# Two transformer-like layers on one core: the residual stream with tokens on the partitions

## The chip, the cores and the metric

The kernel runs on one core of a Trainium2 chip. The metric is the time of one execution on the device in microseconds; lower is better. The time before is the median of three runs. A core has TensorE (PE) for matrix products, VectorE (DVE), ScalarE (ACT) and GpSimd (POOL) for work on tiles, SyncE (SP), which here only issues transfers, and 16 DMA engines move data between device memory (DRAM) and the on-chip buffer. Each engine works through its own list of instructions in order.

## The reference

Input `x` is 512 tokens of width 1024 in fp32; two layers run one after the other. What matters here:

```
def rms_norm(x, g):
    y = x * rsqrt(mean(x * x, axis=-1) + 1e-6)
    return y * g
mod = cond @ mod_w + mod_b            # 6 x 1024 per layer
shift1, scale1, gate1, shift2, scale2, gate2 = split(mod, 6)
h = rms_norm(x, attn_pre_g) * (1 + scale1) + shift1
proj = h @ w_in                       # to four mixers A, B, C, D
y = concat([y_a, y_b, y_c, y_d]) @ w_out
x = x + gate1 * rms_norm(y, attn_post_g)
h = rms_norm(x, mlp_pre_g) * (1 + scale2) + shift2
y = square(relu(h @ mlp_w1)) @ mlp_w2         # 1024 -> 4096 -> 1024
x = x + gate2 * rms_norm(y, mlp_post_g)
```

The mixers are sparse attention with a top-k choice of keys (A), retention (B), gated linear attention (C) and differential attention (D). Each norm is over the 1024 values of one token.

## The kernel before

Every fp32 matrix is split on the chip into a high part (a cast on ACT to a shortened fp32) and a low part (a subtraction on DVE or POOL), and every product is three matmuls (`mm3`, lines 268 to 270). `prep` (line 254) loads a weight tile of 256 KB through SP, casts it (line 262) and subtracts (line 264).

A layer has two functions. `mixers` projects `h` and runs A to D; its output is `yv`, with the width on the partitions, eight tiles of 128 x 512 tokens. `rest` (from line 1231) does everything behind: the output projection (products named `po`), the post-norm and the residual, the pre-norm, and the MLP in four quarters of 1024 hidden channels: `pf` is the first matrix of a quarter, `p2` (shown in the profile as `p`) the second, which adds up in the tiles `y`. The first quarter's `pf` and the whole of the last quarter's `p2` work in two halves of 256 tokens, all else on 512.

The residual `x` and all `y` have the width on the partitions, too: tile `i` holds channels 128 i to 128 i + 127 for all tokens. Then a norm's sum over the width goes across partitions. `SumSq` (line 443) squares each tile on ACT, adds the squares on DVE or POOL into a few partial sums, and adds those over the partitions by a matmul with a matrix of ones (line 467, `sspost` and `sspre`); its result has the sum on all partitions, and `rstd` makes the factor from it on 128 x 256 values. `residual` updates `x`, `prenorm` and `normed` make the normed `h` (lines 510 to 515), in steps that the code places between the products of the next half. `xsave` holds `x` in DRAM while the next layer's mixers use its space.

The modulation `cond @ mod_w` is a list of matrix-vector products on DVE, each with a tile of 512 KB (`gw`, line 281), kept in `todo`; `fill(n)` takes the next n of them at points in the code. `gain` (line 301) combines their results with a norm's weight, 128 x 8 numbers with the width on the partitions.

A list scheduler sets the order of each engine's instructions at build time, from the code's order and its own costs; the table `PLAN` holds choices for it, such as which engine takes a low part. On the chip an instruction starts when the one ahead of it on its engine and its inputs are done.

The lines that the change replaces first of all:

```
ps = yp.tile([P, HT], F32, name="ss" + self.name, tag="yp")
for i, q in enumerate(self.all):
    pe.matmul(ps, ones, q, start=i == 0, stop=i == len(self.all) - 1)
```

Of the kernel before, what the change touches and what calls it, by code (L numbers as in the profile page):

```python
# [39 lines left out]
 'fA': {},  # L40
# [49 lines left out]
P = 128  # L90
L = 2
# [106 lines left out]
def tile_trunk(ctx: ExitStack, tc: tile.TileContext, a, out, dbg=None):  # L198
# [110 lines left out]
    xsave = nc.dram_tensor("xsave", (P, KT, T), F32, kind="Internal").ap()  # L309
# [133 lines left out]
    class SumSq:  # L443

        def __init__(self, name):
            self.n, self.name = 0, name
            self.acc = {}
            self.all = []

        def add(self, t):  # L450
            k = PLAN["sq"][self.n:self.n + 1]
            new = k in "T" or k not in self.acc
            if new:
                q = nt.tile([P, HT], F32, name=f"sa{self.name}{self.n}", tag="sa", bufs=4)
                self.all.append(q)
                self.acc[k] = q
            else:
                q = nt.tile([P, HT], F32, name=f"sq{self.name}{self.n}", tag="sq")
            act.activation(q, t, AF.Square)  # L459
            if not new:  # L460
                (pool if k == "P" else dve).tensor_tensor(self.acc[k], self.acc[k], q, ALU.add)  # L461
            self.n += 1

        def total(self):
            ps = yp.tile([P, HT], F32, name="ss" + self.name, tag="yp")
            for i, q in enumerate(self.all):
                pe.matmul(ps, ones, q, start=i == 0, stop=i == len(self.all) - 1)  # L467
            return ps

# [4 lines left out]
    def h_tiles(name):  # L474
        return [tuple(hp.tile([P, T], F32R, name=f"{name}{i}{s}", tag="h" + s, bufs=KT) for s in "hl") for i in range(KT)]
# [6 lines left out]
    def chain(*gens):  # L482
        for g in gens:
            yield from g

    def step(g, n):
        for _ in range(n):
            next(g, None)

    def residual(l, which, y, ss, half, nxt=None):  # L490

        name = f"{which}{l}_{half}"
        c = cs(half)
        r = rstd(ss.total(), name)
        yield
        g = gmul[l, which]
# [902 lines left out]
```

## Time and profile before

| | |
|---|---|
| three runs | 1503.92, 1506.04, 1510.22 us, median 1506.04 |
| the profiled execution | 1500.35 us |
| its span, first to last instruction | 1498.6 us |
| TensorE busy | 1424.6 us, 95% |
| VectorE busy | 990.7 us, 66% |
| ScalarE busy | 742.3 us, 50% |
| GpSimd busy | 280.5 us, 19% |
| mean granted TensorE clock | 0.981 of full speed |

All views below are of that one profiled execution; times in them count from the first instruction. A name such as `po<-yT_6l,whi` is the tile written and the tiles read, without their numbers; `<-` behind an idle time names what ended it. In the view by stage the busy times stand in the order PE, PEld (TensorE's weight load), DVE, ACT, POOL. "Granted clock" is the share of TensorE's full speed that the chip gave. The stretches of the program, read from the names in the timeline: start and first projections 0 to 55 us, mixers of layer 0 to 330, output projection to 387, first `pf` to 439, the rest of the MLP to 712, the last quarter's `p2` to 764, first projections of layer 1 to 810, its mixers to 1068, output projection to 1118, first `pf` to 1171, the rest of the MLP to 1437, the last quarter's `p2` to 1485, and the end.

### The profile page before, as it was taken

To read this page: it belongs to the slowest core of one execution; us is meant where nothing else is said; L and a number is where in the kernel's file an instruction comes from. 1 tells how busy PE (TensorE), PEld (TensorE's weight loads), DVE (VectorE), ACT (ScalarE), POOL (GpSimd) and SP (SyncE) were. 2 spreads that over 40 slices of the span, in tenths; PEclk is the share of its full clock that TensorE was granted. 3 is DMA by queue.
4 is the path that set the end of the run, shared out by engine and by line. 5 is a ranking of instruction groups with operands and counts; after the bars stand their busy time and mean duration, and the time that the engine had idled before them with its cause. 6 is when DMAs were issued, how large, how long until landed. Compare 5 with 4: busy or idle time off the path is not lost.

```text
span 1498.6 us, 23592 instructions
## 1 busy us (share of the span) xinstructions
PE 1424.6 (95%) x8514; PEld 1190.9 (79%) x8514; DVE 990.7 (66%) x2209; ACT 742.3 (50%) x1655; POOL 280.5 (19%) x268
## 2 busy tenths in 40 slices
PE   7989999999999999999989899999999999999996
PEld 4667878768898878888978769787789888888896
DVE  8798878786796875434477999753678334343435
ACT  4667486656453323324257575855765333242322
POOL 3244321335100000000032443213430000000001
PEclk8999999999999999999999999999999999999999
DMA  9420223466078884333131102211531433333301
GB/s 340 140 68 14 78 71 99 150 205 222 29 245 288 294 268 155 92 99 92 43 113 59 57 15 72 71 43 56 163 104 52 126 93 94 97 97 93 94 20 57
DMA packets 82269, 171.12 MB, mean 114 GB/s; under 512 B 9284, under 2 KB 16102, under 8 KB 81896
## 3 DMA queue, kind: packets, MB, share of 16 engines
q1 hardware_dynamic: 79524, 167.47, 35.7%
q10 hardware_dynamic: 2628, 2.14, 0.4%
q8 instruction: 67, 1.10, 0.3%
q14 instruction: 50, 0.41, 0.1%
HBM read 165.39 MB, written 4.19 MB: 113 GB/s over the span
## 4 chain that ended last, share of the span: by engine, by line
PE 71%; DVE 17%; ACT 4%; DMA 4%; issue 2%; POOL 1%; SPq 0%; DVEq 0%; ACTq 0%; POOLq 0%
PE p L269 7%; PE p L270 7%; PE p L268 7%; PE pf L269 7%; PE pf L270 7%; PE pf L268 7%; PE ptm L268 3%; PE ptm L269 3%; PE ptm L270 3%; DVE ia L797 2%; DVE m L810 2%; DVE ia L811 2%; PE first L1186 1%; DMA gw<-modw 1%; PE firstk L1186 1%
## 5 line engine op out<-in xcount | busy, mean ns | idle before, releaser
L262 ACT CAST whi<-raw 128x512 fp32r<-128x512 f32 x388 | 237.3, 621 | 355.9 <-PE p L269 157.9
L264 DVE TENSOR_TENSOR wlo<-raw,whi 128x512 fp32r<-128x512 f32 x266 | 190.8, 722 | 205.7 <-ACT whi L262 194.1
L264 POOL TENSOR_TENSOR wlo<-raw,whi 128x512 fp32r<-128x512 f32 x122 | 165.1, 1371 | 330.0 <-ACT whi L262 279.7
L461 POOL TENSOR_TENSOR sapost<-sapost,sqpost 128x256 f32<-128x256 f32 x16 | 12.3, 771 | 671.6 <-ACT sqpost L459 671.6
L281 DVE CUSTOM_DVE_ANT_0 gw<-gw,cond 128x1024 f32<-128x1024 f32 x80 | 101.3, 1269 | 40.6 <-DMA gw<-modw 40.2
L810 DVE MAX8 m<-ia 128x8 f32<-128x256 f32 (+2 forms) x96 | 53.1, 556 | 1.3
L811 DVE MATCH_REPLACE8 ia<-m,ia 128x256 f32<-128x256 f32 (+2 forms) x96 | 52.0, 542 | 0.0
L914 ACT COPY QF<-q 32x256 f32<-32x256 f32 x120 | 48.4, 403 | 5.5 <-DVE q L891 2.5
L1288 DVE TENSOR_TENSOR rf<-rf,pf 128x512 f32<-128x512 f32 (+1 forms) x80 | 45.8, 574 | 2.6 <-ACT rf L1287 2.5
L1287 ACT ACTIVATE rf<-pf 128x512 f32<-128x512 f32 (+1 forms) x80 | 40.5, 507 | 5.6 <-PE pf L270 5.6
L923 PE MATMUL sg<-QF,KF 128*64 128x256 f32 x224 | 30.5, 395 | 11.0 <-DVE AC L929 8.2
L602 DVE CUSTOM_DVE_ANT_0 sD<-sd,msk 128x128 f32<-128x128 f32 (+3 forms) x64 | 29.6, 488 | 16.8 <-PE sd L1021 12.0
L604 ACT ACTIVATE sD<-sD,mnD 128x128 f32<-128x128 f32 (+3 forms) x64 | 35.5, 559 | 6.8 <-DVE mnD L602 6.4
L890 POOL TENSOR_TENSOR KF<-F,kc 128x512 f32<-128x512 f32 x16 | 23.9, 1502 | 43.7 <-ACT F L883 42.4
L268 PE MATMUL p<-hd_7h,whi 128*128 128x512 f32 (+1 forms) x80 | 28.6, 358 | 3.1 <-ACT hd_7h L471 3.1
L923 PEld LDWEIGHTS sg<-QF,KF 128*64 128x64 f32 x224 | 14.6, 137 | 21.0 <-issue 13.7
L269 PE MATMUL pf<-h_5l,whi 128*128 128x512 f32 (+1 forms) x80 | 28.0, 350 | 2.8 <-DVE h_5l L515 2.8
L797 DVE SCALAR_TENSOR_TENSOR ia<-rl,wi,ia 128x256 f32<-128x256 f32 (+2 forms) x42 | 29.0, 708 | 2.2 <-ACT rl L791 1.0
L269 PE MATMUL p<-hd_7l,whi 128*128 128x512 f32 (+1 forms) x80 | 28.3, 353 | 0.6 <-DVE hd_7l L472 0.6
L268 PE MATMUL ptm<-whi,h_0h 128*128 128x256 f32 x74 | 25.4, 345 | 3.5 <-ACT h_0h L511 3.5
L467 PE MATMUL sspre<-sapre,ones 128*128 128x256 f32 x48 | 17.3, 474 | 12.0 <-POOL sapre L461 7.1
L268 PE MATMUL p<-hd_0h,whi 128*128 128x512 f32 (+1 forms) x80 | 28.4, 355 | 0.0
(623 smaller groups left out, 5002.2 us busy)
## 6 DMA issues: line engine op xcount, KB each, us to landing
raw<-w SPq DMA_DIRECT2D x256, 256.0 KB, 2.7
gw<-modw SPq DMA_DIRECT2D x80, 512.0 KB, 4.2
raw<-wtm SPq DMA_DIRECT2D x76, 256.0 KB, 2.8
gs<-modw SPq DMA_DIRECT2D x16, 512.0 KB, 6.3
raw<-wo SPq DMA_DIRECT2D x32, 256.0 KB, 2.7
raw<-wtc SPq DMA_DIRECT2D x24, 256.0 KB, 2.8
xin<-xT SPq DMA_DIRECT2D x8, 256.0 KB, 3.5
wq<-wtm SPq DMA_DIRECT2D x8, 256.0 KB, 6.4
```

Source lines behind the costliest of these rows:

```text
L262: act.copy(hi, raw)
L264: (lo_eng or dve).tensor_tensor(lo, raw, bits(hi), ALU.subtract)
L268: pe.matmul(ps, l[0], r[0], start=start, stop=False)
L269: pe.matmul(ps, l[0], r[1], start=False, stop=False)
L270: pe.matmul(ps, l[1], r[0], start=False, stop=stop)
L281: return dve.tensor_tensor_reduce(raw, raw, cond, 1.0, 0.0, ALU.mult, ALU.add, modT[l][:, c:c + 1])
L797: e.scalar_tensor_tensor(t, rl, wi[:, b, hd:hd + 1], t, ALU.mult, ALU.add)
L810: dve.max(m8, acc)
L811: dve.match_replace(acc, m8, acc, MARK)
L914: f(Q[r, :, hd, :], QS4[c // 2][r, 2 * (c % 2):2 * (c % 2) + 2, :])
L923: pe.matmul(ps[t, i], KF[:, lv, t], Q[:, i, :, t], start=True, stop=True)
L1288: dve.tensor_tensor(rl, rl, ps, ALU.mult)
```

## The change

`x` and `y` now have the tokens on the partitions: four blocks of 128 tokens by 1024. The output projection and `p2` use a block of activations as the operand that stands still, and a row of weights of 512 columns as the one that moves; the weights lie in DRAM accordingly. A norm's sum is then along the free dimension: ACT squares two halves of 512 and sums them in the same instruction (`rsqrt_mean`), and the factor is one number a partition. The post-norm's gain has to lie along the free dimension, the same on all partitions: `gain_row` writes the 128 x 8 numbers to DRAM and reads them back as a row for all partitions. What the projections and `pf` need is still the width on the partitions: `turn_block` transposes a normed block on TensorE, eight pieces of 128 x 128, and ACT applies gain and shift while reading the result. `h` is one tile for all eight width tiles (two with the low part). The matrix-vector products that stood in the output projection of layer 0 are emptied ahead of it, eight of them by the plan's entry `fA` within the mixers.

```
- 'fA': {},
+ 'fA': {'2': 2},
...
-    o["wo"] = f("w_out").reshape(L, 2, 4, P, KT, P).transpose(0, 4, 1, 3, 2, 5)
+    o["wo"] = f("w_out").reshape(L, KT, P, 2, T).transpose(0, 3, 1, 2, 4)
...
-    o["w2"] = f("mlp_w2").reshape(L, 4, 2, 4, P, KT, P).transpose(0, 1, 5, 2, 4, 3, 6)
+    o["w2"] = f("mlp_w2").reshape(L, 4, KT, P, 2, T).transpose(0, 1, 4, 2, 3, 5)
...
     def h_tiles(name):
-        return [tuple(hp.tile([P, T], F32R, name=f"{name}{i}{s}", tag="h" + s, bufs=KT) for s in "hl") for i in range(KT)]
+        a, b = (hp.tile([P, KT, T], F32R, name=f"{name}{s}", tag="h" + s, bufs=1) for s in "hl")
+        whole[name] = (a, b)
+        return [(a[:, i], b[:, i]) for i in range(KT)]
...
+    def rsqrt_mean(halves, name):
+        ss = tiny("ss" + name, 2)
+        for c in range(2):
+            junk = nt.tile([P, T], F32, name=f"jk{name}{c}", tag="nm_r", bufs=1)
+            act.activation(junk, halves[c], AF.Square, accum_out=ss[:, c:c + 1])
+        m = tiny("ms" + name)
+        dve.tensor_tensor(m, ss[:, 0:1], ss[:, 1:2], ALU.add)
+        dve.tensor_scalar(m, m, 1.0 / DM, EPS, ALU.mult, ALU.add)
+        r = tiny("rs" + name)
+        act.activation(r, m, AF.Ln)
+        act.activation(r, r, AF.Exp, scale=-0.5)
+        t = tiny("tt" + name)
+        dve.tensor_tensor(t, r, r, ALU.mult)
+        dve.scalar_tensor_tensor(t, t, -0.5, m, ALU.mult, ALU.mult)
+        dve.scalar_tensor_tensor(r, t, 1.5, r, ALU.add, ALU.mult)
+        return r
...
+    def gain_row(l, which):
+        g = gmul[l, which]
+        row = nt.tile([P, DM], F32, name=f"row_{which}{l}", tag="row", bufs=1)
+        d = rows[2 * l + (which == "post2")]
+        sp.dma_start(d.rearrange("k p -> p k"), g)
+        sp.dma_start(row, d.rearrange("k p -> (k p)").unsqueeze(0).broadcast_to([P, DM]))
+        return row
+
+    def add_block(x, src, ys, row, name):
+        for c in range(2):
+            dve.tensor_tensor(ys[c], src[c], row[:, hs(c)], ALU.mult)
+        r = rsqrt_mean(src, name)
+        for c in range(2):
+            dve.scalar_tensor_tensor(x[:, hs(c)], ys[c], r, x[:, hs(c)], ALU.mult, ALU.add)
+
+    def norm_block(x, name):
+        r = rsqrt_mean([x[:, hs(c)] for c in range(2)], name)
+        xn = []
+        for c in range(2):
+            xn.append(nt.tile([P, T], F32, name=f"xn{name}{c}", tag="rs", bufs=RS))
+            act.mul(xn[c], x[:, hs(c)], r)
+        return xn
+
+    def turn_block(l, which, sh_part, b, xn, parts, name):
...
+        for c in range(2):
+            pt = tr.tile([P, 4, P], F32, name=f"tx{name}{c}", tag="tr")
+            v = nt.tile([P, 4, P], F32, name=f"vx{name}{c}", tag="sq")
+            for i in range(4):
+                pe.transpose(pt[:, i], xn[c][:, P * i:P * i + P], ident)
+            for i in range(4):
+                k = 4 * c + i
+                act.activation(v[:, i], pt[:, i], AF.Identity, scale=g[:, k:k + 1], bias=sh[:, k:k + 1])
+            hi, lo = (q[:, 4 * c:4 * c + 4, t] for q in parts)
+            act.copy(hi, v)
+            last = dve.tensor_tensor(lo, v, bits(hi), ALU.subtract)
...
+        fill(len(todo))
+        gain(l, "post1")
+        row = gain_row(l, "post1")
...
+        for b in range(NB):
+            ps = []
+            for c in range(2):
+                ps.append(acc(f"po{l}_{b}_{c}", T))
                 for n, k in enumerate(order):
...
+                    mm3(ps[c], (yT[k][0][:, tb(b)], yT[k][1][:, tb(b)]), wo[c][k], n == 0, n == KT - 1)
+            if b:
+                turn(b - 1)
+            add_block(X["x"][b], ps, y[b], row, f"po{l}_{b}")
+            xn[b] = norm_block(X["x"][b], f"pn{l}_{b}")
...
+                for c in range(2):
+                    wk = [prep(a["w2"][l, q, c, k], [P, T]) for k in range(KT)]
+                    for b in range(NB):
+                        ps = acc(f"p2{l}_{q}_{c}_{b}", T)
+                        for k in range(KT):
+                            mm3(ps, (hid[k][0][:, tb(b)], hid[k][1][:, tb(b)]), wk[k], k == 0, k == KT - 1)
```

The last quarter's `p2` runs in the same way over blocks and column halves, followed per block by `add_block`, and by `norm_block` and `turn` for the next layer, or by two output transfers of 256 KB.

TensorE's list in the output projection of layer 0, before: near the end of the fifth tile of the second half (`po_4_1`) stand ones-products for the pre-norm of the first half (`sspre_0`).

```order
L270 MATMUL po_4_1_4489<-yT_3h,wlo_3995 128x256
L467 MATMUL sspre_0_4522<-sapre_00_4373,ones 128x256
L467 MATMUL sspre_0_4522<-sapre_03_4445,ones 128x256
L268 MATMUL po_5_1_4536<-yT_0h,whi_4005 128x256
L269 MATMUL po_5_1_4536<-yT_0l,whi_4005 128x256
L270 MATMUL po_5_1_4536<-yT_0h,wlo_4007 128x256
L467 MATMUL sspre_0_4522<-sapre_06_4487,ones 128x256
L467 MATMUL sspre_0_4522<-sapre_07_4520,ones 128x256
```

After, at the end of the projection: `txp_20` are the transposes of the third block (first half of the width), `po_3_1` the last block's second column half, `pf_0_0_0` the first tile of the MLP on the first 256 tokens.

```order
L270 MATMUL po_3_1_4395<-wlo_4041,yT_h 128x512
L271 MATMUL po_3_1_4395<-whi_4039,yT_l 128x512
L522 MATMUL txp_20_4420<-ident,xnpn_20_4366 128x128 x4
L269 MATMUL pf_0_0_0_4510<-h_h,whi_4500 128x256
L269 MATMUL pf_0_1_0_4552<-h_h,whi_4542 128x256
L269 MATMUL pf_0_2_0_4594<-h_h,whi_4584 128x256
L269 MATMUL pf_0_3_0_4636<-h_h,whi_4626 128x256
L269 MATMUL pf_0_4_0_4702<-h_h,whi_4692 128x256
L270 MATMUL pf_0_0_0_4510<-h_l,whi_4500 128x256
L271 MATMUL pf_0_0_0_4510<-h_h,wlo_4502 128x256
L269 MATMUL pf_0_0_0_4510<-h_h,whi_4500 128x256
L522 MATMUL txp_21_4432<-ident,xnpn_21_4368 128x128 x4
```

The ones-products are gone, transposes stand at the end of a block's products or between the first products of the MLP, and the first products of five `pf` tiles come one after another.

DVE's list in the mixers of layer 0, before, with the rotary steps of the indexer (`r1I`, `r2I`, `tI`):

```order
L732 TENSOR_TENSOR hlk_2_559<-tK_2_245,hlk_2_559 128x128
L559 TENSOR_TENSOR r1I_1_609<-tI_1_248,ccA 128x128
L560 TENSOR_TENSOR r2I_1_610<-tI_1_248,ssA 128x8x8
L561 TENSOR_TENSOR r2I_1_610<-tI_1_248,ssA 128x8x8
L562 TENSOR_TENSOR tI_1_248<-r1I_1_609,r2I_1_610 128x8x16
L559 TENSOR_TENSOR r1I_2_633<-tI_2_249,ccA 128x128
L560 TENSOR_TENSOR r2I_2_634<-tI_2_249,ssA 128x8x8
L561 TENSOR_TENSOR r2I_2_634<-tI_2_249,ssA 128x8x8
```

After, at the same place, matrix-vector products (`gw_2_1`, `gw_2_2`) stand among them:

```order
L563 TENSOR_TENSOR r1I_1_595<-tI_1_234,ccA 128x128
L564 TENSOR_TENSOR r2I_1_596<-tI_1_234,ssA 128x8x8
L565 TENSOR_TENSOR r2I_1_596<-tI_1_234,ssA 128x8x8
L282 ISA gw_2_1_1977,modT_108<-gw_2_1_1977,cond 128x1024
L282 ISA modT_108 128x1
L736 TENSOR_TENSOR hlk_2_545<-tK_2_231,hlk_2_545 128x128
L736 TENSOR_TENSOR hlk_3_562<-tK_3_232,hlk_3_562 128x128 x2
L566 TENSOR_TENSOR tI_1_234<-r1I_1_595,r2I_1_596 128x8x16
L282 ISA gw_2_2_2117,modT_108<-gw_2_2_2117,cond 128x1024
L282 ISA modT_108 128x1
```

The same rotary steps now come behind two such products; five more stand within the next 71 rows, and one 26 rows ahead.

SP's list in the MLP of layer 0, third and fourth quarter, before: `gw` are matrix-vector tiles of 512 KB, `raw<-w` weight tiles of 256 KB.

```order
L279 DMA gw_4_3_6624<-modw 128x1024
L260 DMA raw_6498<-w 128x512
L279 DMA gw_4_4_6669<-modw 128x1024
L260 DMA raw_6537<-w 128x512
L279 DMA gw_4_5_6714<-modw 128x1024
L260 DMA raw_6543<-w 128x512
L279 DMA gw_4_6_6759<-modw 128x1024
L260 DMA raw_6582<-w 128x512
```

After:

```order
L280 DMA gw_4_2_6336<-modw 128x1024
L261 DMA raw_6255<-w 128x512
L280 DMA gw_4_3_6381<-modw 128x1024
L280 DMA gw_4_4_6426<-modw 128x1024
L280 DMA gw_4_5_6471<-modw 128x1024
L280 DMA gw_4_6_6516<-modw 128x1024
L280 DMA gw_4_7_6561<-modw 128x1024
L280 DMA gw_5_0_6639<-modw 128x1024
L280 DMA gw_5_1_6642<-modw 128x1024
L280 DMA gw_5_2_6671<-modw 128x1024
```

Eight matrix-vector tiles now follow each other, where they took turns with weights.

## Rows read from the trace of the kernel before

**Rows 1.** Page, busy us (share of the span) and count, by engine.
```profile
PE 1424.6 (95%) x8514; PEld 1190.9 (79%) x8514; DVE 990.7 (66%) x2209; ACT 742.3 (50%) x1655; POOL 280.5 (19%) x268
```

**Rows 2.** By stage: us, busy us (count) per engine, clock, DMA share, GB/s.
```profile
55.00:181.00 126.00, 113.99 (x775) 91.69 (x773) 116.48 (x304) 84.47 (x214) 54.18 (x54) 0.97 0.20 60
330.00:387.00 57.00, 52.83 (x409) 50.33 (x408) 39.31 (x71) 34.31 (x80) 22.31 (x18) 0.97 0.57 186
387.00:439.00 52.00, 49.28 (x399) 48.05 (x399) 47.51 (x105) 27.81 (x67) 4.42 (x4) 1.00 0.38 121
529.00:573.00 44.00, 40.28 (x162) 31.91 (x161) 33.16 (x57) 10.78 (x18) 0.00 (x0) 0.92 0.86 273
536.00:542.40 6.40, 5.78 (x13) 4.21 (x14) 5.63 (x10) 1.10 (x2) 0.00 (x0) 0.50 0.90 287
712.00:764.00 52.00, 50.94 (x411) 49.58 (x410) 29.82 (x67) 18.72 (x43) 7.38 (x9) 1.00 0.13 41
764.00:810.00 46.00, 38.26 (x269) 36.06 (x269) 30.83 (x80) 26.00 (x73) 14.75 (x14) 0.89 0.35 103
1068.00:1118.00 50.00, 48.07 (x386) 46.56 (x386) 31.48 (x56) 32.44 (x75) 20.85 (x18) 1.00 0.53 165
1118.00:1171.00 53.00, 50.27 (x407) 49.00 (x406) 43.65 (x96) 31.21 (x75) 4.41 (x4) 1.00 0.27 79
1171.00:1437.00 266.00, 266.00 (x1152) 215.86 (x1151) 106.54 (x161) 89.85 (x152) 0.00 (x0) 1.00 0.33 94
1440.00:1460.00 20.00, 20.00 (x172) 20.00 (x172) 4.20 (x10) 2.92 (x7) 1.47 (x2) 1.00 0.00 1
```

**Rows 3.** Waits of PE, 330 to 440 us: us in total, times, longest.
```profile
PE sspre L467 <- DVE sapre L461: 3.4, 1, 3.4
PE sspre L467 <- POOL sapre L461: 1.8, 2, 1.3
```

**Rows 4.** Waits of PE, 712 to 812 us.
```profile
PE sspre L467 <- POOL sapre L461: 4.0, 2, 3.0
PE ptm L268 <- ACT h_0h L511: 3.5, 1, 3.5
```

**Rows 5.** The last ones-products: ns least/median/most, first and last start.
```profile
L467 PE MATMUL sspost<-sapost,ones x8: 378/379/379, 1484.5 to 1486.0; 128*128 128x256 f32 x8
```

**Rows 6.** Timeline of PE, 216.9 to 217.5 us: start, us, what.
```profile
216.92 0.66 PE L618 MATMUL tpD<-ident,sD 128*128 128x128 f32 x4 [0.19 <-ACT QD L657]
```

**Rows 7.** Groups of ACT by form: busy us, mean ns | idle before.
```profile
L604 ACT ACTIVATION_READ_ACCUMULATOR sD<-sD,mnD 128x1 f32 x64 | 12.2, 191 | 0.0
...
L334 ACT ACTIVATE first_sq<-xin 128x512 f32<-128x512 f32 x8 | 4.6, 621 | 1.7 <-DMA xin<-xT 1.7
...
L731 ACT CAST hlk<-tK 128x128 fp32r<-128x128 f32 x16 | 4.2, 319 | 1.6 <-DVE tK L562 1.6
```

**Rows 8.** Waits of DVE, 55 to 181 us.
```profile
DVE r1K L559 <- ACT tK L716: 4.4, 1, 4.4
```

**Rows 9.** Groups of DVE by form.
```profile
L281 DVE CUSTOM_DVE_ANT_0 gw<-gw,cond 128x1024 f32<-128x1024 f32 x80 | 101.3, 1269 | 40.6 <-DMA gw<-modw 40.2
...
L1319 DVE TENSOR_TENSOR ym<-ym,p 128x512 f32<-128x512 f32 x16 | 11.0, 687 | 21.8 <-PE p L270 21.8
...
L608 DVE RECIPROCAL rcD<-suD 128x1 f32<-128x1 f32 x64 | 9.9, 159 | 8.3 <-ACT sD L604 7.6
```

**Rows 10.** Group of POOL, low parts of weights.
```profile
L264 POOL TENSOR_TENSOR wlo<-raw,whi 128x512 fp32r<-128x512 f32 x122 | 165.1, 1371 | 330.0 <-ACT whi L262 279.7 <-PE ptc_t L270 13.8 <-PE ix L779 12.5
```

**Rows 11.** Timeline of the last 14 us.
```profile
1484.45 1.89 PE L467 MATMUL sspost<-sapost,ones 128*128 128x256 f32 x8
...
1491.54 4.41 SPq L1358 DMA_DIRECT2D yT<-x  x4
```

**Rows 12.** DMA issues: KB each, us to landing (a view of them all).
```profile
yT<-x SPq DMA_DIRECT2D x8, 256.0 KB, 2.2
...
c_pos<-pos ACTq DMA_DIRECT2D x1, 2.0 KB, 3.6
```

More of the change, by code (lines that the diff above doesn't have):

```diff
@@ L307, in gain @@
         gmul[l, which] = g
[L309 removed]
+    xsave = nc.dram_tensor("xsave", (NB, P, DM), F32, kind="Internal").ap()
+    rows = nc.dram_tensor("rows", (2 * L, KT, P), F32, kind="Internal").ap()
     X = {}
@@ L441, in cs @@
         return slice(HT * half, HT * half + HT)
[L443 to L468, printed above, removed]
     def split(v, hi, lo, eng=None):
@@ L480, in run_all @@
                 pass
[L482 to L495, printed above, removed]
-        g = gmul[l, which]
-        for i in range(KT):
-            x = X["x"][i][:, c]
-            dve.tensor_tensor(y[i][:, c], y[i][:, c], r, ALU.mult)
-            dve.scalar_tensor_tensor(x, y[i][:, c], g[:, i:i + 1], x, ALU.mult, ALU.add)
-            if nxt is not None:
-                nxt.add(x)
-            yield
@@ L517, in prenorm, with tiny @@
-    def prenorm(l, which, sh_part, half, h, ss):
-        name = f"{which}{l}_{half}"
-        r = rstd(ss.total(), name)
-        yield
-        for i in range(KT):
-            last = normed(l, i, X["x"][i], gmul[l, which][:, i:i + 1], modT[l][:, 8 * sh_part + i:8 * sh_part + i + 1],
-                          r, h[i], cs(half), name)
-            yield
+    vs = []
+    def tiny(name, n=1):
+        return nt.tile([P, 2], F32, name=name, tag="tn", bufs=8)[:, :n]
+    def rsqrt_mean(halves, name):
[14 more added lines that the diff above has]
+        return r
@@ new lines, in rest, with tb, y_blocks @@
+        X["x"] = [xp.tile([P, DM], F32, name=f"x{l}_{b}") for b in range(NB)]
+        for b in range(NB):
+            sp.dma_start(X["x"][b], a["xt"][b] if l == 0 else xsave[b])
+        def tb(b):
+            return slice(P * b, P * b + P)
+        def y_blocks(name):
+            m = yb.tile([P, 4, T], F32, name=f"{name}_m", tag="ym", bufs=1)
+            o = [yb.tile([P, T], F32, name=f"{name}_{i}", tag="y", bufs=4) for i in range(4)]
+            return [[m[:, 0], m[:, 1]], [m[:, 2], m[:, 3]], o[:2], o[2:]]
@@ new lines, in rest @@
+            parts = whole[f"h1{l + 1}_"]
+            turn = lambda b: turn_block(l + 1, "pre1", 0, b, xn[b], parts, f"p1{l}_{b}")
+        ws = [[prep(a["w2"][l, 3, c, k], [P, T]) for k in range(KT)] for c in range(2)]
+        for b in range(NB):
+            for c in range(2):
+                ps = acc(f"p2{l}_3_{b}_{c}", T)
+                for k in range(KT):
+                    mm3(ps, (hid[k][0][:, tb(b)], hid[k][1][:, tb(b)]), ws[c][k], k == 0, k == KT - 1)
+                dve.tensor_tensor(y[b][c], y[b][c], ps, ALU.add)
+            if turn and b:
+                turn(b - 1)
+            x = X["x"][b]
+            gy = [nt.tile([P, T], F32, name=f"gy{l}_{b}{c}", tag="rs", bufs=RS) for c in range(2)]
+            add_block(x, y[b], gy, row, f"p2{l}_{b}")
+            if turn:
+                act.dma_start(xsave[b], x)
+                xn[b] = norm_block(x, f"p1n{l}_{b}")
+            else:
+                for c in range(2):
+                    sp.dma_start(out[b][:, hs(c)], x[:, hs(c)])
@@ L1359, in rest @@
+        ch = (lambda: turn(NB - 1)) if turn else None
         stk.close()
@@ L1362, in rest @@
         return h, ch
-    def save(half):
-        c = cs(half)
-        for i in range(KT):
-            act.dma_start(xsave[:, i, c], X["x"][i][:, c])
-        yield
     h, ch = h_tiles("h10_"), None
```

137 lines of the change are left out of this document (38 added, 99 removed).

## The prediction

> **What bounds the kernel now.** First the page's busy line: TensorE is busy for 1424.6 us, 95% of the span [rows 1]. A change can gain what TensorE does besides the products that must be, and what it waits; I read all else as "does it keep TensorE waiting". Next the table of busy time by stage [rows 2]: the MLP quarters of layer 1 are solid (266 us busy of 266, 1152 products of 512 columns, 0.231 us each). TensorE's idle time sits where layers and norms meet: 330 to 439 us (output projection and first MLP quarter of layer 0), 1068 to 1171 (the same of layer 1), 712 to 810 (last quarter of layer 0, first projections of layer 1). Its waits there [rows 3, 4] show why: a ones-product for a sum of squares waits for partial sums of DVE or POOL (3.4, 1.8 and 4.0 us), and the next layer's first projection for the normed activations (3.5 us). One stage is different: from 55 to 181 us DVE is busy for 116.5 of 126 us and sets the pace. [...]
>
> The profiled execution took 1500.35 us (span 1498.6 and 1.75 around it); the timed runs have a median of 1506.04. I sum against 1500.35 and add the difference of 5.7 us at the end.
>
> **Matmuls.** 384 products of 256 columns become 192 of 512 in four places (output projection and last MLP quarter, two layers). At 256 columns 172 start in 20 us, 0.1163 us each [rows 2], so 44.7 us; 192 at 0.231 are 44.3. That is 0.4 us a place and counted inside the stages below. The other MLP quarters only swap which operand stands still.
>
> **Ones-products out, transposes in.** 56 ones-products go: 16 around each output projection, 16 at the layer boundary, 8 at the end. One is two records, and eight records start within 1.5 us [rows 5], so 0.43 us each, 6.9 us for 16. 96 transposes of 128x128 come, 32 at each of three places; four took 0.66 us from first start to last end [rows 6]. A start alone costs between 0.10 and 0.165 us; I take 0.12, so 3.8 us a place.
>
> **Output projection and first MLP quarter.** The new chain for a block of 128 tokens runs beside the next block's 48 products, 48 x 0.231 = 11.1 us of cover. Its length from rows: two Squares with accumulator reads on ACT, 2 x (0.62 + 0.19) [rows 7]; five tiny steps on DVE and two on ACT, nearest rows 0.16 (DVE, 128x1) [rows 9] and 0.32 (ACT, 128x128) [rows 7], together at most 1.5; two updates of x on DVE, 2 x 0.69 [rows 9]; Squares and tiny steps once more, 3.1; two scalings on ACT, 2 x 0.62. Sum 8.8 us if every engine is free. But ACT works in order and also has, per block, 8 Identities of 128x128 and two casts of the block before (8 x 0.32 + 2 x 0.62 = 3.8 us) and the casts of the next weights. I take 12 to 14 us, so that a block is late by 1 to 3 us.
>
> [...]
>
> The first MLP product has no cover at all. The normed activations are one tile now, in the space that held the mixer output, so no cast may write them before the last product of the projection has read that space. Then come, in ACT's order, a cast, Identities that waited for one of two buffers, more casts, and DVE's subtractions: 4 x 0.62 + 8 x 0.32 + 0.69 = 5.7 us, of which I count 4 to 7 as TensorE's wait, and 2 to 3 for the half clock behind it (6.4 us at 0.50 cost 3.2) [rows 2]. At the start all 16 weight tiles are wanted within one block, 11 us, where each pair had 2.8 us of products before; a low part on POOL takes 1.37 us [rows 10]: 3 us of stall. Sum of stalls 9 to 17, I take 13 in layer 0 and 12 in layer 1. Layer 0: 109 us (330 to 439) become 44.3 + 44.7 + 3.8 + 13 = 106, gain 3. Layer 1: 103 us become 105, loss 2. With stalls of 6 or 20 us each the pair gives +14 or -15.
>
> **Layer boundary.** 712 to 810 is 98 us: 44.7 of MLP products, 6.9 of ones-products, 28 of projections (240 of 256 columns), and 18 of waits and half clock (granted clock 0.89 on average in its second half) [rows 2, 4]. After: 44.3 + 28 + 3.8 + stalls. Only the last block's chain has no products of its own stage beside it, and there the projections of the first three blocks stand; I take 8 us of stalls, 84 in all. Gain 14, bounds 6 (stalls of 16) and 20 (stalls of 2).
>
> **Tail.** Last product, 1484.45 (ones-products begin behind it), to the end at 1498.6 [rows 11]. After: last add 0.69, row product 0.69, Square 0.81, tiny steps 1.5, x 1.4, an output DMA of 2.2 [rows 12], the hand-overs between them and the program's end: 9 to 11 us. The stretch from 1437 on is 61.6 us before and 44.3 + 10 = 54.3 after. Gain 7, bounds 4 and 9.
>
> **Early matrix-vector products.** The plan's `fA` and the fill moved ahead of the projection put eight more of DVE's 128x1024 products into the mixers of layer 0, 8 x 1.27 = 10.2 us [rows 9], in the stage where DVE sets the pace. A wait of DVE of 4.4 us for ACT [rows 8] may take some, and two or three rounds of top-k now stand behind the first softmax. I take a loss of 5, bounds 0 and 10. In the projection, where they stood, TensorE's products hid them: nothing comes back there.
>
> **Gain rows.** Four times SP writes 128x8 numbers to DRAM in pieces of 4 bytes and reads one row back to all partitions. The nearest row is 2 KB in 3.6 us, and 256 KB in 2.2 [rows 12]: 4 to 8 us for the pair. In three places dozens of SP's transfers lie between write and read; in the first, SP waits with it for the gain and weights of the mixers queue behind. I count nothing, at most 3 us. [...]
>
> Sum: 3 - 2 + 14 + 7 - 5 = 17. 1500.35 - 17 = 1483, and 5.7 more for the median of runs: **1488 us**.
>
> **Rivals.** *Eaten: the chain is longer than its cover.* With a chain of 16 us instead of 13 the three blocks that have a follower are later by 3 us each, in two layers 18 us, and 1488 + 18 = 1506 is no change. For it: some ten hand-overs between engines in each chain, and ACT, busy for 34 of 57 us in this stage already [rows 2]. Against it: the transposes may stand a block later in TensorE's order, as they do for the block before last.
>
> *Slower: the weights come in bursts.* The second MLP matrix is fetched as eight tiles of a column half, all wanted before the first block's sum ends, and in one place SP now issues eight matrix-vector tiles of 512 KB in a row, where weights and such tiles took turns. From 529 to 573 us the queues are busy for 0.86 and move 273 GB/s [rows 2]: eight tiles, 4.2 MB, are 15 us, in which no weight comes. If the weights ahead last for 5 of them, TensorE waits for 10, and pays some 3 more at half clock. Two such places and the full price of the early products are 2 x 13 + 5 = 31 us; against what TensorE loses there now, 3.7 us of wait and 3.2 of half clock [rows 2], 24 more: 1512. It decides from 18 us lost in this way on. For it: TensorE waits in this very stretch already. Against it: the bytes are the same, and from 387 to 439 us the queues are busy for 0.38 only.
>
> *More is gained.* If the casts behind the projections keep TensorE waiting for 3 us alone and the boundary for 2, little half clock follows: 6 us less in each of three places, 1470.
>
> *It does not do what it says* is excluded for the ones-products: TensorE's order holds none.
>
> **Chances.** Forecast 0.45 (its own range 1478 to 1498), more gained 0.15, eaten 0.2, slower 0.2. The range goes from 1466 to 1513. About 0.5%, 7.5 us, is what a measurement of this kernel tells from no change. Faster: forecast and more gained, 0.6, and a little of the eaten case: 0.61. Same 0.2, slower 0.19.
>
> **What would show it.** Right: a boundary of 84 us; the output DMA about 8 us behind the last product; DVE full from 55 to some 186 us; the first MLP product of each layer waiting for a cast or its low part for 4 to 7 us, the clock at 0.50 behind it. Wrong: waits of TensorE for the input of the transposes at every block (chain longer than cover), waits for weights of over 10 us between 440 and 575 us (bursts), or the stages of 109 and 103 us outside 98 to 113 (my stalls).

## The result: slower by 1.1%, and the profile after

The changed kernel took 1522.89 us (median, 1520.66 to 1525.20) against 1506.43 us before in the same job: ratio 1.0107, 95% interval 1.0081 to 1.0134. The forecast was 1488 us, faster; the time lies above its range of 1466 to 1513, on the side of the rival "slower".

The profiled execution took 1525.2 us, its span 1523.4, so 24.8 us more than before. The first lines to read are the page's busy line and the packets (columns as in [rows 1]).

```profile
PE 1420.2 (93%) x7730; PEld 1148.0 (75%) x7730; DVE 947.6 (62%) x2119; ACT 759.0 (50%) x1739; POOL 250.7 (16%) x234
...
DMA packets 83094, 173.13 MB, mean 114 GB/s; under 512 B 13188, under 2 KB 15910, under 8 KB 82728
```

TensorE is busy for 4 us less and the program 25 us longer: the time is in waits. The busy times by stage, the stages cut where the product names change (columns as in [rows 2]):

```profile
335.00:394.50 59.50, 50.41 (x215) 39.14 (x213) 34.44 (x67) 36.37 (x91) 16.97 (x13) 0.96 0.47 143
394.50:442.60 48.10, 48.10 (x398) 48.10 (x398) 34.90 (x75) 29.32 (x75) 1.30 (x1) 0.97 0.46 150
531.80:601.80 70.00, 51.40 (x194) 38.13 (x193) 44.65 (x75) 14.65 (x25) 0.00 (x0) 0.83 0.75 218
735.30:782.00 46.70, 46.70 (x210) 37.78 (x209) 23.53 (x57) 24.75 (x68) 1.34 (x2) 1.00 0.14 51
782.00:814.00 32.00, 21.14 (x143) 20.38 (x142) 16.05 (x35) 20.14 (x58) 6.72 (x5) 0.84 0.41 124
1203.20:1470.90 267.70, 267.70 (x1153) 216.11 (x1152) 106.89 (x161) 90.33 (x153) 0.00 (x0) 1.00 0.32 94
...
540.50:564.40 23.90, 10.33 (x19) 5.78 (x20) 18.79 (x32) 4.92 (x9) 0.00 (x0) 0.50 0.85 268
```

The third row is the loss: 194 products need 70.0 us where a stage of that size in layer 1 needs 45. The last row lies inside it: the granted clock was 0.50 for 23.9 us, with TensorE busy for less than half of them. In the kernel before, the same stage took 51.4 us:

```profile
527.80:579.20 51.40, 47.68 (x194) 37.82 (x193) 38.22 (x68) 12.02 (x20) 0.00 (x0) 0.93 0.79 248
```

Stage by stage, with the forecast's own terms:

| stretch | before | after | change | forecast |
|---|---|---|---|---|
| start and mixers of layer 0 | 329.6 | 335.0 | +5.4 | +5 |
| output projection and first `pf`, layer 0 | 109.6 | 107.7 | -1.9 | -3 |
| second products of quarter 1, layer 0 | 51.4 | 69.9 | +18.5 | 0 |
| rest of the MLP of layer 0 up to the last `p2` | 221.8 | 222.8 | +1.0 | 0 |
| last `p2` of layer 0, first projections, to the mixers' first long wait | 139.8 | 140.1 | +0.3 | -14 |
| rest of the mixers of layer 1 | 213.5 | 218.6 | +5.1 | 0 |
| output projection and first `pf`, layer 1 | 105.3 | 109.0 | +3.7 | +2 |
| rest of the MLP of layer 1 | 266.3 | 267.8 | +1.5 | 0 |
| last `p2` and the end | 61.4 | 52.5 | -8.9 | -7 |

Two terms failed: 18.5 us in one stage for which nothing was counted, and a gain of 14 us at the layer boundary that did not come. Where TensorE waits in these two, 525 to 580 us and 782 to 815 us (us in total, times, longest):

```profile
PE p L271 <- DVE hd_4l L447: 7.1, 1, 7.1
PE p L269 <- ACT hd_7h L446: 3.4, 1, 3.4
PE p L269 <- ACT hd_5h L446: 3.3, 1, 3.3
PE p L269 <- ACT hd_6h L446: 3.2, 1, 3.2
```

```profile
PE ptm L269 <- ACT ca L723: 6.8, 1, 6.8
PE ptm L269 <- ACT whi L263: 3.2, 1, 3.2
PE ptm L270 <- POOL wlo L265: 0.9, 1, 0.9
```

The names in the first are hidden activations, but their makers are not the cause. The chain of what ended last, cut to that stretch (start, us, what), shows transfers of matrix-vector tiles, for which DVE waits in its order ahead of the activations:

```profile
519.02 4.94 DMA gw<-modw
...
530.47 10.80 DMA gw<-modw
...
542.66 4.23 DMA gw<-modw
...
548.29 4.25 DMA gw<-modw
```

One of them took 10.8 us instead of some 4. SP's own timeline and the view of the tile `rows` say what lay in front of it: four writes of the gain in pieces of 4 bytes, the second at 454.73 and the third at 528.91 us.

```profile
454.73 0.43 SPq L493 DMA_DIRECT2D rows<-g_post  x1
457.43 0.33 SPq L280 DMA_DIRECT2D gw<-modw  x1
466.91 0.33 SPq L494 DMA_DIRECT2D row_post<-rows  x1
```

The write was issued at 454.7 and SP could issue the read-back at 466.9. Each of the four took 11.1 to 12.0 us to land. Meanwhile (10 us stretches, columns as before, the last two DMA share and GB/s) the queues were busy without moving much:

```profile
440.00:450.00 10.00, 10.00 (x56) 8.54 (x56) 8.63 (x19) 5.45 (x12) 0.00 (x0) 1.00 0.86 282
450.00:460.00 10.00, 10.00 (x44) 8.07 (x43) 3.71 (x7) 1.02 (x2) 0.00 (x0) 1.00 0.73 211
460.00:470.00 10.00, 10.00 (x44) 8.02 (x44) 1.75 (x3) 2.64 (x5) 0.00 (x0) 1.00 0.78 77
...
530.00:540.00 10.00, 5.47 (x23) 3.77 (x21) 4.08 (x8) 3.54 (x7) 0.00 (x0) 1.00 0.89 123
```

A share of 0.78 with 77 GB/s, beside 0.86 with 282: while small pieces pass, the queues are busy with little. Most of that is not the pieces' own time. From 455.5 to 466.5 us their packets of 4 bytes took about 9 ns each, 9.5 us in sum over the 16 queues; the 187 large packets among them, of 4 KB, took 0.66 us on average, where 0.16 us is the median of such packets in this execution and 0.13 the mean of those of 2 and 4 KB together. The pieces hold up the transfers beside them.

### The profile page after: what moved, and what is told of

It is laid out like the page before. It is cut to its first block, busy times and chain, and to the rows that moved or that the text cites. A ratio compares the mean times of both kernels' runs of the same rounds, so it can differ in the third digit from the quotient of the medians.

```text
span 1523.4 us, 21884 instructions
## 1 busy us (share of the span) xinstructions
PE 1420.2 (93%) x7730; PEld 1148.0 (75%) x7730; DVE 947.6 (62%) x2119; ACT 759.0 (50%) x1739; POOL 250.7 (16%) x234
## 4 chain that ended last, share of the span: by engine, by line
PE 70%; DVE 15%; ACT 6%; issue 4%; DMA 4%; POOL 1%; SPq 0%; ACTq 0%; DVEq 0%; POOLq 0%
PE p L271 8%; PE p L269 8%; PE p L270 8%; PE pf L269 7%; PE pf L270 7%; PE pf L271 7%; PE ptm L269 3%; PE ptm L270 3%; PE ptm L271 3%; DMA gw<-modw 3%; DVE ia L814 2%; DVE m L813 2%; ACT whi L263 1%; DVE ia L800 1%; PE ptc_t L271 1%
## 5 line engine op out<-in xcount | busy, mean ns | idle before, releaser
L270 PE MATMUL pf<-h_l,whi 128*128 128x512 f32 (+1 forms) x640 | 223.3, 349 | 0.0
L269 PE MATMUL pf<-h_h,whi 128*128 128x512 f32 (+1 forms) x640 | 223.3, 351 | 0.0
L271 PE MATMUL pf<-h_h,wlo 128*128 128x512 f32 (+1 forms) x640 | 223.0, 349 | 0.0
L269 PE MATMUL ptm<-whi,h_h 128*128 128x256 f32 x592 | 176.7, 299 | 10.0 <-ACT ca L723 6.8
L270 PE MATMUL ptm<-wlo,h_h 128*128 128x256 f32 x592 | 173.3, 293 | 0.9 <-POOL wlo L265 0.9
L271 PE MATMUL ptm<-whi,h_l 128*128 128x256 f32 x592 | 172.3, 291 | 0.0
L269 PEld LDWEIGHTS pf<-h_h,whi 128*128 128x128 f32 x640 | 121.4, 191 | 16.9 <-ACT h_h L527 0.2
L271 PEld LDWEIGHTS pf<-h_h,wlo 128*128 128x128 f32 x640 | 121.1, 189 | 16.8
L270 PEld LDWEIGHTS pf<-h_l,whi 128*128 128x128 f32 x640 | 121.1, 189 | 16.7
L270 PEld LDWEIGHTS ptm<-wlo,h_h 128*128 128x128 f32 x592 | 116.7, 197 | 6.3 <-issue 4.8
```

The lines of the kernel that those rows point to most:

```text
L269: pe.matmul(ps, l[0], r[0], start=start, stop=False)
L270: pe.matmul(ps, l[0], r[1], start=False, stop=False)
L271: pe.matmul(ps, l[1], r[0], start=False, stop=stop)
```

## The experiments

Each kernel was timed against the kernel before on the same chip; "span" is that of its profiled execution (before 1498.6, changed kernel 1523.4 us).

**Where do the 18.5 us come from: pieces, SP's wait, or the order of the loads?** Both edits below begin from the changed kernel. The first makes the row on TensorE, the second does so too and still issues the writes.

```
-        sp.dma_start(d.rearrange("k p -> p k"), g)            # second kernel: this line stays
-        sp.dma_start(row, d.rearrange("k p -> (k p)").unsqueeze(0).broadcast_to([P, DM]))
+        for c in range(2):
+            gb = nt.tile([P, 4, P], F32, tag="sq")
+            act.copy(gb, g[:, 4 * c:4 * c + 4].unsqueeze(2).broadcast_to([P, 4, P]))
+            pt = tr.tile([P, 4, P], F32, tag="tr")
+            for i in range(4):
+                pe.matmul(pt[:, i], gb[:, i], ident, start=True, stop=True)
+            act.copy(row[:, hs(c)], pt.rearrange("p k q -> p (k q)"))
```

> The gain rows are made on TensorE (eight 128x128 products with the identity for each row, copied by ScalarE), so that the four writes of 128x8 numbers in pieces of 4 bytes and the four read-backs are gone; all else as in the changed kernel. Theory A (the pieces): each write keeps the DMA queues busy for some 11 us and SP waits for it, and this starves the stretch from 440 to 600 us. Then the second products of quarter 1 in layer 0, 70.1 us in the changed kernel, take 46 to 53 us, and the kernel 1500 to 1508 us. Theory B (the order): the runs of matrix-vector tiles ahead of weights starve it, and they stay as they are here. Then the stage stays at 65 to 70 us, the kernel at 1517 to 1523.

Measured: 1508.66 us, ratio to before 1.0017 (0.9996 to 1.0039), span 1503.6; the stage took 54.1 us. SP's order of weight and matrix-vector tiles was the same but for the missing rows and a few tiles that moved by a place or two; runs of up to eight matrix-vector tiles are still there.

> As the kernel with rows made on TensorE, but the four writes in pieces of 4 bytes are still issued at their places; nothing reads what they write, and SP waits for none of them. If the pieces' hold on the queues is what costs, the stage of 70.1 us comes back to 58 to 70 us and the kernel to 1512 to 1522 us. If SP's wait between write and read-back is what costs, both stay as without the writes: 46 to 53 us, and 1500 to 1508.

Measured: 1525.40 us, ratio 1.0128 (1.0093 to 1.0163), span 1525.5; the stage took 73.4 us. The stage and one stretch of 10 us behind the second write, with the writes and, below, without:

```profile
460.00:470.00 10.00, 10.00 (x44) 8.04 (x43) 1.23 (x2) 3.66 (x6) 0.00 (x0) 1.00 0.84 90
532.40:605.80 73.40, 52.12 (x194) 38.51 (x193) 43.43 (x74) 14.54 (x25) 0.00 (x0) 0.79 0.71 208
```

```profile
460.00:470.00 10.00, 10.00 (x45) 8.01 (x44) 6.03 (x11) 1.46 (x3) 0.00 (x0) 1.00 0.73 228
529.80:583.80 54.00, 47.91 (x194) 37.17 (x193) 35.50 (x63) 11.54 (x20) 0.00 (x0) 0.94 0.71 234
```

With the writes 90 GB/s pass at a share of 0.84, without them 228 at 0.73. SP waits for no write in the second kernel, so SP's wait is not it: what the pieces do to the queues costs 16.7 us by the medians of the two kernels (1525.40 and 1508.66), 19.3 us in this stage of the profiled executions. The cause is that of theory A, though both kernels came out somewhat slower than it had them (54.1 us against 46 to 53, 73.4 against 58 to 70). For theory B, the order of the loads, little is left: 54.1 us is 2.7 more than the kernel before took here, and the other 6.4 us above 45 were lost there already.

**The rest of that stage.** The first kernel below has the rows on TensorE and the low parts of three weight groups of layer 1 on DVE (`'blo': 'dddd'`, see the boundary). The second adds this:

```
-            dve.tensor_tensor(rl, rl, ps, ALU.mult)
+            fence[:] = [dve.tensor_tensor(rl, rl, ps, ALU.mult)]     # no later gw ahead of this
...
-                            dve.tensor_tensor(y[b][c], y[b][c], ps, ALU.add)
-                        fill(2)
+                            fence[:] = [dve.tensor_tensor(y[b][c], y[b][c], ps, ALU.add)]
+                        fill(2 if q == 2 else 1)
```

> Both edits that helped in one kernel: rows made on TensorE, and the low parts of layer 1's first three weight groups on DVE. If the two act in different places their gains add: 16 us in quarter 1 of layer 0 and some 8 us at the layer boundary, 1498 to 1503 us, a little below the kernel before. If the queue stretch takes back what the boundary gives, 1505 to 1510.

Measured: 1499.22 us, ratio 0.9931 (0.9905 to 0.9957), span 1494.1. The gains add; the stage still takes 54.8 us.

> As the kernel with both edits, and the 56 matrix-vector products of layer 0's MLP tied to places over all four quarters, so that SP loads their tiles between weights up to 735 us instead of up to 600. If the density of the transfers from 440 to 600 us makes what is left of the wait in quarter 1 (54 us with the rows on TensorE, 44.5 to 45 without a wait), this stage falls to 45 to 47 us and the kernel by 7 to 10 us: 1489 to 1495. If the wait moves to a later quarter or to the boundary, which needs the last of them, nothing or less than 3 us is gained.

Measured: 1490.35 us, ratio 0.9875 (0.9847 to 0.9902), span 1488.5: the best kernel. The stage has no wait left:

```profile
530.70:575.80 45.10, 45.10 (x194) 36.22 (x193) 23.16 (x39) 9.19 (x15) 0.00 (x0) 1.00 0.50 161
```

At a share of 0.50 instead of 0.71 DVE's tiles come in time. The edit changed two things together: with 8 matrix-vector products in this stage instead of 19 in the two kernels with rows on TensorE above there are fewer transfers (a tile lands in 3.5 us instead of 4.2, medians), and fewer such products stand ahead of the activations in DVE's order. Which of the two took away what was left of the wait was not separated. How much of this gain belongs to the new layout? The same spreading in the kernel before:

> The kernel before (tokens on the free axis, ones-products) with the same spreading of the 56 matrix-vector products of layer 0's MLP over all four quarters. It lost 3.7 us of wait and 3.4 us of half clock at 533 us. If these come from the density of the transfers, the spread kernel gains them: 1499 to 1502 us against 1506 to 1509, and what the tokens on the partitions are worth beside equal edits is the difference to the best kernel, 8 to 12 us. If nothing is gained here (1505 to 1509), the spreading only repairs what the new order of w2 brought, and the layout is worth all of the best kernel's gain.

Measured: 1498.70 us, ratio 0.9956 (0.9942 to 0.9970). The spreading alone brings 0.4%; the best kernel stands at 0.9875. But that kernel also has the low parts on DVE, which was not tried in the kernel before; with the low parts as they were, rows on TensorE and spreading give 0.9919 (the last kernel of the boundary, below). So the layout with a row that costs no transfers is worth 0.4 to 0.8% beside the spreading.

**The layer boundary.** In the changed kernel TensorE waits there for a copy named `ca`: it frees one of the two tiles for the sums of the next layer's projections in PSUM (the memory in which the kernel puts the results of its products), and stands in ScalarE's order behind the last block's scaling (start, us, what):

```profile
799.95 1.33 ACT L511 ACTIVATE xnp1n<-x,rsp1n 128x512 f32<-128x512 f32 x2 [1.93 <-DVE rsp1n L482]
801.19 0.19 ACT L721 COPY Va<-ptm 128x64 f32<-128x64 f32 x1
801.28 0.17 ACT L722 ACTIVATE wi<-ptm 128x8 f32<-128x8 f32 x1
801.36 0.17 ACT L723 COPY ca<-ptm 128x16 f32<-128x16 f32 x1
```

The chain before it, from the last product at 782.1 to the scaled block at 801.3, took 19.2 us where I had 12 to 14. Steps of DVE on 128x1 numbers, and POOL beside them:

```profile
797.38 0.15 DVE L480 TENSOR_TENSOR ttp1n<-rsp1n 128x1 f32<-128x1 f32 x1
797.42 2.48 POOL L265 TENSOR_TENSOR wlo<-raw,whi 128x512 fp32r<-128x512 f32 x2 [3.49 <-ACT whi L263]
...
797.56 1.14 DVE L481 SCALAR_TENSOR_TENSOR ttp1n<-ttp1n,msp1n 128x1 f32<-128x1 f32 x1
...
798.74 1.18 DVE L482 SCALAR_TENSOR_TENSOR rsp1n<-ttp1n,rsp1n 128x1 f32<-128x1 f32 x1
```

The edit `'blo': 'dppd'` to `'dddd'` takes POOL away from there.

> The changed kernel with the low parts of layer 1's first three weight groups on DVE instead of two in four on POOL. Theory A: POOL's subtractions hold DVE's steps on 128x1 numbers (1.2 us beside one, 0.16 without), and this makes the last block's chain at the layer boundary long; without them TensorE's waits there, 3.2, 0.9 and 6.8 us, fall to under 6 together and the kernel gains 4 to 8 us: 1515 to 1519. Theory B: ScalarE's order, which has the evictions of the first projections behind the chain, makes the waits whatever the length: they stay at 9 us or more, the kernel within 2 us of 1523.

Measured: 1514.62 us, ratio 1.0054 (1.0026 to 1.0082), span 1515.8. From the start of the last second product of layer 0 to the start of the output projection of layer 1 it took 302.6 us instead of 312.4, and the wait of 6.8 us is gone. But the edit moved ScalarE's order as well: the copies now stood ahead of the chain, and the chain itself was hardly shorter (18.1 us). Two more kernels set the two apart. One keeps POOL and puts the copies first (the last block's norm is written behind them, its Squares held by a scheduling dependency); the other keeps POOL out and holds the copies behind the scaling.

```
+            hold[:] = evicted[-1:]                       # kept POOL: Squares behind the copies
+            xn[NB - 1] = norm_block(X_last, f"p1n{l}_{NB - 1}")
...
+            i = act.copy(ca[:, b, 0:16], ps[:, 200:216])     # POOL out: copies behind the scaling
+            if l and b < 2:
+                after(muls[-1], i)
```

> The changed kernel with POOL's low parts as they are, but in ScalarE's order at the layer boundary the copies that free the first two PSUM tiles of the next layer's projections stand ahead of the last block's Squares instead of behind its scaling. (The kernel with the low parts on DVE had moved ScalarE's order too, and its last chain was about as long as before: the two causes are mixed there.) Theory B, ScalarE's order: TensorE's wait of 6.8 us goes to under 2 us, the stretch from the last second product of layer 0 to the output projection of layer 1 from 312.8 to 302 to 306 us, the kernel to 1514 to 1518. Theory A, POOL's hold on DVE's tiny steps: they are still there, so the wait stays over 5 us and the kernel within 2 us of 1523.

Measured: 1524.05 us, ratio 1.0101 (1.0077 to 1.0124), span 1523.6, the stretch 311.4 us. Theory B misses. Of theory A the time came true, not the wait of over 5 us: it is 3.0 now, and the waits in the stretch are

```profile
PE ptm L269 <- ACT whi L263: 3.2, 1, 3.2
PE ptm L269 <- ACT ca L725: 3.0, 1, 3.0
PE ptm L270 <- POOL wlo L265: 0.9, 1, 0.9
```

> The counterpart: low parts on DVE (POOL does not run beside the chain), but the last of the copies that free those two PSUM tiles held behind the last block's scaling on ScalarE, as in the changed kernel. Theory B: the wait of some 6 us is back and the stretch is 310 to 315 us, the kernel 1521 to 1525. Theory A: the stretch stays at 303 to 306 us, the kernel at 1513 to 1517.

Measured: 1521.22 us, ratio 1.0094 (1.0070 to 1.0119), span 1524.7, the stretch 309.1 us. Theory A misses here: POOL is out, and a wait of 6.3 us is back.

```profile
PE thk L742 <- ACT hlk L737: 6.3, 1, 6.3
```

It is not the wait for the copies themselves. ScalarE's order there also puts key casts (`hlk`) behind the Ln and Exp of the chain, and TensorE's order has their transposes (`thk`) ahead of the next tile of the projections; the copies would have come later still, at 804.5 us, behind the scaling.

So neither is the cause alone. With the copies first and POOL at work, they still stand behind weight casts that wait for tiles (the stretch 311.4 us); with POOL out and the copies last, TensorE waits for what ScalarE does behind the chain (309.1). Only with both changed do the 10 us go (302.6, against 312.4 with neither). Whether POOL acts through DVE's short steps or through weights that come late was not separated.

> Candidate for the best: rows made on TensorE, the 56 matrix-vector products spread over four quarters, POOL's low parts kept, and the evictions first. If ScalarE's order was the cause at the boundary it is as fast as the kernel with the low parts on DVE, 1488 to 1493 us; if POOL's hold was, 5 to 8 us slower.

Measured: 1496.65 us, ratio 0.9919 (0.9891 to 0.9947): 6 us slower than the kernel with the low parts on DVE, as expected for the case that POOL matters; its stretch is 312.8 us. That agrees with the kernel that has the copies first.

**Does a POOL instruction hold DVE's short steps?** Four POOL multiplications were put beside the very last chain, which nothing covers:

```
+            if (l, b) == (L - 1, NB - 1):
+                xn_dm = nt.tile([P, T], F32, name="dm", tag="sq")
+                for i in range(4):
+                    pool.tensor_tensor(xn_dm, y[b][1], y[b][0], ALU.mult)
```

> The changed kernel with four added POOL multiplications of 128x512 into a scratch tile, made to start together with the very last block's norm chain, which nothing covers; their result is not used. Theory A: a step of DVE on 128x1 numbers beside a POOL instruction waits until that ends, 1.2 us instead of 0.16. Then the chain from the last product to the end, 7.6 us, becomes 10 to 13 us and the kernel 1525 to 1528. Theory B: what was slow at the layer boundary was ScalarE's order only. Then the last chain stays at 7.6 to 8 us, the kernel at 1522 to 1523.

Measured: 1527.63 us, ratio 1.0113 (1.0081 to 1.0145), beside 1522.89 for the changed kernel: by the times alone unclear. The chain shows it: 11.0 us from the last product (1516.2) to the end (1527.2) instead of 7.6.

```profile
1517.07 5.72 POOL L1348 TENSOR_TENSOR dm<-ym,ym 128x512 f32<-128x512 f32 x4 [355.33 <-DVE ym L1340]
...
1517.77 1.01 DVE L474 TENSOR_TENSOR msp<-ssp 128x1 f32<-128x1 f32 x1
1518.82 0.15 DVE L475 TENSOR_SCALAR msp<-msp 128x1 f32<-128x1 f32 x1
...
1519.47 0.65 DVE L480 TENSOR_TENSOR ttp<-rsp 128x1 f32<-128x1 f32 x1 [0.50 <-ACT rsp L478]
1520.16 0.16 DVE L481 SCALAR_TENSOR_TENSOR ttp<-ttp,msp 128x1 f32<-128x1 f32 x1
1520.35 1.11 DVE L482 SCALAR_TENSOR_TENSOR rsp<-ttp,rsp 128x1 f32<-128x1 f32 x1
1521.50 2.50 DVE L503 SCALAR_TENSOR_TENSOR x<-gy,rsp,x 128x512 f32<-128x512 f32 x2
```

Three of five short steps and the update of `x` (2.5 us for the pair, 1.4 in the changed kernel) are late. It is a hold until the POOL instruction ends, not a share of speed: three of the four POOL instructions end at 1518.77, 1520.11 and 1521.45 us, the three late steps at 1518.78, 1520.12 and 1521.46, and the two quick steps began in the gaps of 0.08 us before the next POOL instruction. It is not every short step: in the changed kernel 14 RECIPROCALs on 128x1 took 0.15 to 0.17 us within a POOL instruction of 128x512. The 16 norm steps that took over 0.5 us in the changed kernel (lines 480 to 482) have two inputs in the on-chip buffer; which property decides was not tried.

**The output projection's chains.** On top of the kernel with rows on TensorE and `blo` on DVE, `'wolo': 'pdpddppp'` became `'dddddddd'`.

> As the kernel with both edits, and the low parts of the output projections' weights on DVE too (ten of sixteen tiles were on POOL). If POOL's hold on DVE's tiny steps lengthens the block chains, TensorE's waits for the transposes' input (2.6 us a layer in the changed kernel) and for POOL's low parts (1.4 us) go: 3 to 8 us less than with the two edits. If DVE has too much to do there (16 x 0.69 us more in 55 us, and the row products), the first block starts later: 0 to 6 us more.

Measured: 1498.57 us, ratio 0.9931 (0.9907 to 0.9956), the same as without. In layer 0 projection and first `pf` end 3.4 us earlier, in the mixers of layer 1 and its projection it is lost again: inconclusive on a gain, and no sign that these chains cost much.

**The early matrix-vector products.** `'fA': {'2': 2}` back to `{}`.

> The changed kernel with the plan's entry fA empty: the eight matrix-vector products no longer stand among the first steps of layer 0's mixers but in a run ahead of the output projection. If they cost DVE's time in the mixers (theory A), the output projection of layer 0 starts 4 to 6 us earlier than 335.0 us, and the kernel gains as much unless the late gain row holds the first block: 1517 to 1520 us. If DVE's wait for ScalarE took them for nothing (theory B), the start stays within 1 us of 335.

Measured: 1534.69 us, ratio 1.0200 (1.0166 to 1.0234). Both theories miss: the output projection starts at 345.4 us, 10 us later. At the first top-k softmax TensorE's wait ends 2.9 us earlier (182.1 instead of 185.0 us), so their price among the first steps is some 3 us. The loss lies behind it: ahead of the projection, where these products stand now, TensorE waits for 4.8 us at 285 and for 2.9 at 323; that these two waits come from them was not followed back. So the plan's entry saves more ahead of the projection than it costs among the first steps.

## Why the prediction was wrong

Between the forecast for the profiled execution, 17 us less, and the 24.8 us more lie 41.8 us: 18.5 in quarter 1 of layer 0, 14.3 at the layer boundary, 5.1 in the mixers of layer 1, and the rest in small parts.

The step that failed first is "gain rows": "4 to 8 us for the pair", and then "I count nothing, at most 3 us." The write alone takes 11 to 12 us, and it was not SP's wait that mattered, which I weighed, but the 16 queues, which I did not: the writes, two of which lie in or just before that dense stretch, hold up the transfers beside them, and this cost 16.7 us by the medians. The row I took the price from, 2 KB in 3.6 us [rows 12], was a transfer of some other form and measured latency; what was needed is the number of pieces. The prediction names the pieces of 4 bytes, and 128x8 numbers are 1024 of them for each write, but it put no price on them. The packets under 512 B bear the number out: 13124 in the kernel with the rows on TensorE and the writes, 8964 without the writes, so 1040 for each of four, one for each number and 16 more.

The rival "slower: the weights come in bursts" named the right stage and a time, 1512 us, that is 11 us under the measured one, with the half clock as a part of the price; its "from 18 us lost in this way on" was met in size, 18.5 us in this stage. Its cause was wrong, so the nearness is in part luck: the runs of matrix-vector tiles stayed when the rows went to TensorE, and 16 of the 18.5 us went. What may be right in it is that the transfers were dense there already; with the matrix-vector products spread over four quarters the rest went too, but so did most of these products ahead of the activations in DVE's order. I gave it 0.2, and against it I set that "the bytes are the same"; the bytes were not the measure.

The second step is the boundary's "I take 8 us of stalls". Cut as in the prediction, to the 240th product of the projections, the boundary took 97.2 us before and 95.5 after, where 84 was forecast:

```profile
712.30:809.50 97.20, 88.40 (x674) 84.93 (x673) 60.35 (x147) 44.27 (x114) 21.63 (x22) 0.95 0.23 70
735.30:830.80 95.50, 83.84 (x481) 73.65 (x480) 48.09 (x114) 53.08 (x151) 14.05 (x12) 0.95 0.24 75
```

Idle time and half clock came to 16.8 us (11.7 and 5.1), outside the bound of 16, and the 18 us that I had for the kernel before by subtraction were 13.9 (8.8 and 5.1). I had counted the first projections as cover for the last chain. The products of its first three blocks are 168, about 19.5 us, of which 96 stand ahead of the last block's transposes; but their PSUM tiles are freed by ScalarE, in order, behind that chain or behind weight casts, and the cover ended after 13 us, waits included. And the chain took 19 us: ScalarE served the Identities of the block before between its steps, and the DVE steps that I priced at 0.16 us took up to 1.2 beside POOL. Without POOL there the chain still took 18.1 us, so POOL's hold is the smaller part of its length. The hint was there: at the end of the kernel before, DVE steps on 128x256 took 0.41 to 0.43 us with POOL idle and 0.94 beside it, and I read only the transfers of that stretch:

```profile
1489.99 0.94 DVE L1354 TENSOR_TENSOR x<-x,ym 128x256 f32<-128x256 f32 x1
```

Right was the mechanism in the other stages, and the size with some luck. The wait behind each output projection, predicted as 4 to 7 us for casts that must wait for the last product, is 5.7 us in both layers (in layer 0 `po` ends at 388.76 and `pf` starts at 394.49). That it is just the sum of 5.7 is luck: there are a weight cast, two casts and five Identities, but also the end of a block's scaling and a Square that the sum did not have, and in TensorE's order a group of transposes stands in front and takes most of the wait:

```profile
390.06 1.13 ACT L527 CAST h_h<-vxp 128x512 fp32r<-128x512 f32 x2
390.71 1.94 DVE L528 TENSOR_TENSOR h_l<-vxp,h_h 128x512 fp32r<-128x512 f32 x2 [1.21 <-ACT h_h L527]
392.08 1.86 ACT L525 ACTIVATE vxp<-txp,modT,g_pre 128x128 f32<-128x128 f32 x5 [0.30 <-DVE h_l L528]
393.64 1.07 PE L522 MATMUL txp<-ident,xnpn 128*128 128x128 f32 x4 [4.88 <-ACT vxp L525]
```

Idle time and half clock in these stages are 12.5 us in layer 0 and 14.6 in layer 1, where I took 13 and 12, and the stage changes of -1.9 and +3.7 us against -3 and +2 follow from it. The half clock that I priced at 2 to 3 us did stand behind the wait: in layer 0 the granted clock was 0.50 from 393.7 to 397.1 us, a loss of 1.7 us, and in the kernel before the stretch at 0.50 [rows 2] had 3.1 us without a product right ahead of it. The rival "eaten" by long chains did not come there: one wait of 2.6 us a layer for a block's transposes. The mixers' loss of 5.4 against 5 is right in size; some 3 us of it are at the first softmax, and the rest lies behind it, which was not predicted. The tail gained 8.9 instead of 7: hand-overs between engines are 0.03 to 0.05 us, and an Ln or Exp on 128x1 takes 0.20 us, not 0.32. The mixers of layer 1, for which I counted nothing, lost 5.1 us, of which 3.4 is more half clock (5.1 us instead of 1.7) and 1.0 more idle time; why the clock stayed low longer was not tried.

## What to carry to other kernels

Price a small transfer by its pieces and by what shares the queues then, not by its bytes or its landing time: four writes of 4 KB, 1024 pieces each, cost 17 to 19 us here, with two of them where the queues were busy already. When a chain of small steps takes the place of a wide one, look for what the same engines do in between, in their order, and for who frees the buffers of the work that is to cover it. The stretch in which transfers were just fast enough, with the queues busy for 0.79 of it in the kernel before, had little room for more: spreading its loads brought 0.4% in the kernel before and 0.6% in the new one.

## What was not expected of the hardware

- A write of 128x8 numbers in pieces of 4 bytes took 11.1 to 12.0 us, and 77 to 123 GB/s passed beside it at a queue share of 0.78 to 0.89, while the packets of 4 KB took 0.66 us behind the second write and 0.47 behind the third instead of 0.16 (median); a tile of 512 KB behind it took 10.8 us instead of 4.2.
- The norm's DVE steps on 128x1 take 0.157 us (mean of 121 in the changed kernel) with POOL idle and 1.04 us (mean of 19, 16 of them over 0.5) where a POOL instruction of 128x512 runs: those held end when that one ends, within 0.02 us. RECIPROCALs on 128x1 were not held (0.15 to 0.17 us, 14 of them), nor were the products with the gain row, 128x512, which read PSUM (0.69 us with and without, two of them beside POOL).
- Products with 512 moving columns take 45.07 us for 192 when the activations stand still, 44.66 when the weights did: 0.4 us a stage in each of layer 1's first three quarters, which no run here explains.
